# A hybrid attention layer on one core: first tile normalised in halves, rotary queries gated, narrower first scores, an offset added by DMA, the last residual placed in PSUM

## The chip, the core and the metric

The kernel runs on one core of one Trainium2 chip. The metric is device time in microseconds (us) of one execution; lower is better. Columns of a profile row are: start, duration, engine, line of the kernel, operation, output tile <- input tiles, sizes. PE is TensorE (PEld its weight loads), DVE is VectorE, ACT is ScalarE, POOL is GpSimd, SP is SyncE, which here only issues DMAs. A letter q behind an engine's name means its queue.

## The reference, cut to what matters

One decoder layer over 512 tokens with 1024 channels, float32. The input is normalised; gated linear attention and multi-head latent attention run on the same stream, are merged by gates and projected; then come a residual with layer norm (LN1), a squared-ReLU MLP of width 4096, and a residual with layer norm (LN2).

```
h = layer_norm(x, ln_in_g, ln_in_b)
mix = token_mixer(h, cos, sin, w_in, ..., w_q_b, ..., w_out)
h = layer_norm(DEEPNORM_ALPHA * h + mix, ln1_g, ln1_b)
ff = jnp.square(jax.nn.relu(h @ w_ff1)) @ w_ff2
h = layer_norm(DEEPNORM_ALPHA * h + ff, ln2_g, ln2_b)

# latent attention, 8 heads, blocks of 128 queries, block blk reads keys [0, 128 * (blk + 1))
s = einsum(q_nope[q0:q1], k_nope[:q1]) + einsum(apply_rope(q_rope)[q0:q1], k_rope[:q1])
p = softmax(where(mask, s * scale, -inf))
o = einsum(p, v[:q1])
```

## The kernel before, in words

**Number format.** Every large product is done in fp32r, a reduced form of float32. Each operand is split into a high and a low part (hi, lo), and a product is three matmuls: hi by hi, hi by lo, lo by hi. Weights come by DMA on SP's queue into three raw buffers; `pump` (L177) splits them one or two pieces ahead of use: ACT copies the high part (L189, tile whi or xh), DVE subtracts to get the low part (L190, tile wlo or xl). There are two buffers for each part, so a piece's split waits until TensorE has done with the piece two before.

**Order of the work.** The program is written as a main line of matrix products (`gemm_fm`, `gemm_tm`, which put 512 or fewer output columns in one PSUM bank) with side tasks, generators that `tick` moves on by a step between matmuls. The framework then sets each engine's order from a simulated time line and the order of the program. On the chip each engine executes its own list strictly in that order. `tc.issue_after(ins)` holds the instructions of its block behind `ins` if they are on the same engine as `ins`. PSUM has eight banks, four in a pool mm and four in a pool px; ring buffers in SBUF are given by tag. One tag, C, has eight buffers, for h0, qn, PT1, res, bc, T1 and T2.

**Start.** x has four tiles of 128 tokens. Tiles 0 and 1 come first, then the first weights. `ln_in0` (L437) normalises both through `ln_rows` (L400): statistics on DVE (L403, L404), epsilon (L405), the power -1/2 on POOL (L406), then for tile 0 a scalar nmr on DVE (L409) and one ACT instruction of 1024 columns (L410), for tile 1 one DVE instruction (L412). `ln_transpose` (L414) then transposes both tiles on TensorE (L421), 128 channels at a time, and makes h high (ACT, L424) and low (DVE, L428 and L429). The first projection (L278 to L280) follows.

**Rotary queries.** `mla_qr` (L813) projects the rotary part of four heads' queries for four token tiles into two PSUM banks; `ev_qr` (L816) multiplies each tile with cosine and sine on DVE (L498 to L500, reading PSUM), adds on POOL (L501), and splits the sum (L114, L115). The next main product, `y_gla` (L1098, matmuls L245 to L247 on ogT), needs four accumulators, so also the two banks of the queries.

**Scores.** `mla_head` (L859) computes for block i of 128 queries scores against max(128 (i + 1), 256) keys in five fp32r matmuls (L871 to L875), adds the mask by a bf16 matmul (L876), and takes the softmax over 128 (i + 1) keys.

**LN1's residual.** After LN1, `residual1` (L1193) keeps alpha times the normed stream for the second residual: the gain and offset rows bg and bb (tile bc) are multiplied by alpha (L1197, L1198), each of the four res tiles is multiplied by bg (L1199, L1203), and bb is added (L1204), all on DVE. Beside it, `win_sums` (L1234) combines quarters of w_ff2 (L1239) into T1 and T2; its second half takes the two buffers of tag C that bg and bb leave. The MLP's second product, `win_f2` (L1270), adds its results into res by accumulating DMAs from POOL's queue (L1305).

**End.** The last quarter of the second product is done by token tiles. For the last tile, three column groups of 512, 256 and 256 are accumulated (L1413 to L1415); after each, DVE adds the residual in SBUF (L1417) and takes statistics by 256 columns (L1419). `ln2` (L1208) then merges the statistics (L1215), adds epsilon (L1216), takes the power on POOL (L1217), and in two halves computes (r - mean) * gain (L1220) and times the power plus offset (L1221), and sends each half out on SP (L1222).

Of the kernel before, what the change touches and what calls it, by code (L numbers as in the profile page):

```python
# [19 lines left out]
P = 128  # L20
# [32 lines left out]
def tile_hybrid_block(ctx: ExitStack, tc: tile.TileContext, I, out, dbg=None):  # L53
# [23 lines left out]
    def B(shape, dt=F32, n="b"):  # L77
        return pb.tile(shape, dt, tag="B", name=nm(n))

    def S(shape, dt=F32, n="s"):  # L80
        return sm.tile(shape, dt, tag=n, name=nm(n))
# [5 lines left out]
    def MM(n="mm"):  # L87
        return pm.tile([P, T], F32, tag="mm", name=nm(n))
# [121 lines left out]
    def spawn(g):  # L210
        active.append(g)
        return g
# [187 lines left out]
    def ln_rows(src, dst, mv, on_act=False):  # L400
        bst = S([P, 2, 6], F32, "bst")
        for j in range(2):
            nc.vector.bn_stats(bst[:, j, :], src[:, j * T:(j + 1) * T])  # L403
        nc.vector.bn_aggr(mv, bst)  # L404
        vts(mv[:, 1:2], mv[:, 1:2], LN_EPS, None, op0=ALU.add)  # L405
        gtt(mv[:, 1:2], mv[:, 1:2], mhalf[:, 0:1], op=ALU.pow)  # L406
        if on_act:
            nmr = S([P, 1], F32, "nmr")
            stt(nmr, mv[:, 0:1], -1.0, mv[:, 1:2], op0=ALU.mult, op1=ALU.mult)  # L409
            act(dst, src, AF.Identity, scale=mv[:, 1:2], bias=nmr)  # L410
        else:
            vts(dst, src, mv[:, 0:1], mv[:, 1:2], op0=ALU.subtract, op1=ALU.mult)  # L412

# [21 lines left out]
    hT = []  # L435

    def ln_in0():  # L437
        for tt in range(2):
            ln_rows(xt[tt], xt[tt], mvin[:, tt, :], on_act=tt == 0)
        yield from ln_transpose(xt, g_in, b_in, hT, 0, alt=True)  # L440

    pump(-1)
# [370 lines left out]
    def mla_qr(g):  # L813
        qst = []

        def ev_qr(a, j, ps):  # L816
            src = ps[:, :4 * ROPE].rearrange("p (h c) -> p h c", c=ROPE)
            csb = cs2[:, a, None, :].to_broadcast([P, 4, ROPE])
            snb = sn2[:, a, None, :].to_broadcast([P, 4, ROPE])
            t1 = B([P, 4, ROPE], F32, "rt1")  # L820
            t2 = B([P, 4, ROPE], F32, "rt2")
            rope(src, csb, snb, t1, t1, t2)
            q2 = B([P, 4, 2, ROPE], F32R, "q2")
            split(t1, q2[:, :, 0, :], q2[:, :, 1, :], scale=scale)
            qst.append(q2)
        gemm_tm([PL["qr", g]], qlT, 4 * ROPE, ev_qr)

        def tr():
            for h in range(4):
                p = PX(dt=F32R)  # L830
                for tt in range(NT):
                    nc.tensor.transpose(p[:, tt * P:(tt + 1) * P], qst[tt][:, h].rearrange("p a b -> p (a b)"), identr)
                yield
                q = B([P, T], F32R, "QS")
                act(q, f(p), AF.Copy)
                QS[4 * g + h] = q
        return spawn(tr())
# [21 lines left out]
    def mla_head(h, hl, qn, kn, vt):  # L859
        for _ in range((0 if h == MH - 1 else STAG) * hl):  # L860
            yield
        KK, qs = KKs[0], QS[h]
        Ps = []
        P02 = B([P, T], F32, "P02")
        for i in range(NT):
            n = P * (i + 1)
            nn = max(n, 2 * P)
            c = slice(i * P, (i + 1) * P)
            p = PX()
            o = p[:, :nn]  # L870
            mm(o, qn[:, 0, c], kn[:, 0, :nn], start=True, stop=False)  # L871
            mm(o, qn[:, 0, c], kn[:, 1, :nn], start=False, stop=False)
            mm(o, qn[:, 1, c], kn[:, 0, :nn], start=False, stop=False)
            mm(o, qs[:, c], KK[:, 0, :nn], start=False, stop=False)
            mm(o, qs[:, c], KK[:, 1, :nn], start=False, stop=False)  # L875
            mm(p[:, c], identb, negb, start=False, stop=True)  # L876
            mx = S([P, 1], F32, "mx")
            nc.vector.tensor_reduce(mx, p[:, :n], axis=AX.X, op=ALU.max, negate=True)
            Pm = P02[:, :P] if i == 0 else P02[:, P:] if i == 2 else B([P, T], F32, "Pm")
            sme = S([P, 1], F32, "sme")  # L880
            act(Pm[:, :n], p[:, :n], AF.Exp, bias=mx, accum_out=sme)
            nc.vector.reciprocal(sme, sme)
            vts(Pm[:, :n], Pm[:, :n], sme, None, op0=ALU.mult)
            Ps.append(Pm)
            if i != 0:
                yield

        PT = [A([P, 2, T], F32R, "PT0"), A([P, 2, T], F32R, "PT1"), B([P, 2, 256], F32R, "PT2")]
        plan_t = ([(i, 0, i) for i in range(4)], [(i - 1, 1, i) for i in range(1, 4)] + [(3, 3, 3)],
                  [(i - 2, 2, i) for i in range(2, 4)])  # L890
        for b, (pl, pt) in enumerate(zip(plan_t, PT)):
            n = len(pl) * P
            p = PX()
            for cc, j, i in pl:
                nc.tensor.transpose(p[:, cc * P:(cc + 1) * P], Ps[i][:, j * P:(j + 1) * P], ident)
            split(p[:, :n], pt[:, 0, :], pt[:, 1, :])
            if b != 1:
                yield
        PT0, PT1, PT2 = PT
        while vt[NT - 1] is None:  # L900
            yield
        o = PX()
        for j in range(NT):
            c = slice(hl * P, (hl + 1) * P)
            vh, vl = vt[j][:, 0, c], vt[j][:, 1, c]
            if j == 0:
                ph, pl, od = PT0[:, 0, :], PT0[:, 1, :], o
            elif j == 1:
                ph, pl, od = PT1[:, 0, :384], PT1[:, 1, :384], o[:, 128:]
            elif j == 2:  # L910
                ph, pl, od = PT2[:, 0, :], PT2[:, 1, :], o[:, 256:]
            else:
                ph, pl, od = PT1[:, 0, 384:], PT1[:, 1, 384:], o[:, 384:]
            mm(od, vh, ph, start=j == 0, stop=False)
            mm(od, vh, pl, start=False, stop=False)
            mm(od, vl, ph, start=False, stop=j == NT - 1)
        yield
        om = A([P, 2, T], F32R, "omT")
        st["om"] = split(o, om[:, 0, :], om[:, 1, :])
        omT[h] = om  # L920
# [272 lines left out]
    def residual1():  # L1193
        bg, bb = bcast_row("ln1_g"), bcast_row("ln1_b")
        yield
        with tc.issue_after(st["ln"][1].ins):
            vts(bg, bg, ALPHA, None, op0=ALU.mult)  # L1197
            vts(bb, bb, ALPHA, None, op0=ALU.mult)  # L1198
            vtt(res[0], res[0], bg, op=ALU.mult)  # L1199
        yield  # L1200
        for tt in range(NT):
            if tt:
                vtt(res[tt], res[tt], bg, op=ALU.mult)  # L1203
            vtt(res[tt], res[tt], bb, op=ALU.add)  # L1204
            yield


    def ln2(tt, bst=None):  # L1208
        mv = S([P, 2], F32, "mv")
        r = res[tt]  # L1210
        if bst is None:
            bst = S([P, 2, 6], F32, "bst")
            for j in range(2):
                nc.vector.bn_stats(bst[:, j, :], r[:, j * T:(j + 1) * T])
        nc.vector.bn_aggr(mv, bst)  # L1215
        vts(mv[:, 1:2], mv[:, 1:2], LN_EPS, None, op0=ALU.add)  # L1216
        gtt(mv[:, 1:2], mv[:, 1:2], mhalf[:, 0:1], op=ALU.pow)  # L1217
        for j in range(2):
            c = slice(j * T, (j + 1) * T)
            stt(r[:, c], r[:, c], mv[:, 0:1], bg[:, c], op0=ALU.subtract, op1=ALU.mult)  # L1220
            stt(r[:, c], r[:, c], mv[:, 1:2], bb[:, c], op0=ALU.mult, op1=ALU.add)  # L1221
            nc.sync.dma_start(out[tt * P:(tt + 1) * P, c], r[:, c])  # L1222
        yield
# [115 lines left out]
    for ci in range(FC):  # L1339
# [34 lines left out]
        else:  # L1374
# [29 lines left out]
            gemm_tm(PL["f2last"], hid, T, ev_res, tts=(2,))  # L1404
            spawn(ln2(2))
            tt, r, bst = 3, res[3], S([P, 4, 6], F32, "bst4")
            for c0, n in ((0, T), (T, 256), (T + 256, 256)):
                acc = MM()[:, :n]
                ws = slice(c0 % T, c0 % T + n)
                for k in range(nb):  # L1410
                    hi, lo = weights(PL["f2last"][c0 // T], k)
                    xh, xl = hid[k][:, 0, tt * P:], hid[k][:, 1, tt * P:]
                    mm(acc, xh, hi[:, ws], start=k == 0, stop=False)  # L1413
                    mm(acc, xh, lo[:, ws], start=False, stop=False)
                    mm(acc, xl, hi[:, ws], start=False, stop=k == nb - 1)  # L1415
                    tick(None)
                vtt(r[:, c0:c0 + n], acc, r[:, c0:c0 + n], op=ALU.add)  # L1417
                for j in range(c0 // 256, (c0 + n) // 256):
                    nc.vector.bn_stats(bst[:, j, :], r[:, j * 256:(j + 1) * 256])  # L1419
            finish(spawn(ln2(3, bst)))  # L1420


# [46 lines left out]
```

## Time and profile before

| | |
|---|---|
| three runs, us | 896.37, 896.48, 897.16 (median 896.48) |
| the profiled execution, us | 896.5 |
| its span in the profile, us | 894.7 |
| granted TensorE clock | 0.998 |
| first projection matmul, last matmul start, us | 11.62, 887.36 |
| DMA moved | 109.41 MB, mean 122 GB/s |

The span is the time from the first to the last instruction in the trace; 1.8 us of the execution lie around it. The profile lists waits as "engine, tile, line <- engine, tile, line that ended the wait: us in total, times, longest". Ends of matmuls are modelled and overlap their successors, so how close matmuls follow is read from their starts: 512 columns are usually 0.227 us apart, 256 columns 0.12.

### The profile page before, as it was taken

To read this page: it belongs to the slowest core of one execution; us is meant where nothing else is said; L and a number is where in the kernel's file an instruction comes from. 1 tells how busy PE (TensorE), PEld (TensorE's weight loads), DVE (VectorE), ACT (ScalarE), POOL (GpSimd) and SP (SyncE) were. 2 spreads that over 40 slices of the span, in tenths; PEclk is the share of its full clock that TensorE was granted. 3 is DMA by queue.
4 is the path that set the end of the run, shared out by engine and by line. 5 is a ranking of instruction groups with operands and counts; after the bars stand their busy time and mean duration, and the time that the engine had idled before them with its cause. 6 is when DMAs were issued, how large, how long until landed. Compare 5 with 4: busy or idle time off the path is not lost.

```text
span 894.7 us, 12542 instructions
## 1 busy us (share of the span) xinstructions
PE 877.5 (98%) x4796; PEld 760.5 (85%) x4796; DVE 614.5 (69%) x1003; ACT 445.1 (50%) x757; POOL 170.4 (19%) x190
## 2 busy tenths in 40 slices
PE   6999999999999999999999999999999999999996
PEld 5988888888889988888888888988888888889986
DVE  7835855577775745747756797997556646787866
ACT  6455543443546543535645423366457546656810
POOL 1003442444531010100000002103400520141000
PEclk9999999999999999999999999999999999999999
DMA  7314413216325723112207618004950991399312
GB/s 246 122 47 163 131 60 95 71 48 152 84 71 175 197 87 102 49 55 58 95 25 260 210 48 305 3 0 118 314 135 3 271 257 35 76 231 236 117 62 82
DMA packets 73037, 109.41 MB, mean 122 GB/s; under 512 B 7904, under 2 KB 42080, under 8 KB 72976
## 3 DMA queue, kind: packets, MB, share of 16 engines
q1 hardware_dynamic: 57520, 76.62, 27.1%
q0 software_dynamic: 13536, 28.32, 13.8%
q10 hardware_dynamic: 1920, 3.66, 1.2%
q8 instruction: 38, 0.62, 0.3%
q14 instruction: 23, 0.19, 0.1%
HBM read 91.28 MB, written 4.72 MB: 107 GB/s over the span
## 4 chain that ended last, share of the span: by engine, by line
PE 97%; DVE 1%; DMA 1%; ACT 0%; issue 0%; DVEq 0%
PE mm L245 12%; PE mm L247 12%; PE mm L246 12%; PE mm L278 7%; PE mm L279 7%; PE mm L280 7%; PE mm L1030 3%; PE mm L1029 3%; PE mm L1028 3%; PE px L1288 2%; PE px L1287 2%; PE px L1286 2%; PE px L738 2%; PE mm L1288 2%; PE mm L1287 2%; PE mm L1286 2%
## 5 line engine op out<-in xcount | busy, mean ns | idle before, releaser
L190 DVE TENSOR_TENSOR wlo<-wraw,whi 128x1024 fp32r<-128x1024 f32 (+1 forms) x98 | 110.4, 1127 | 110.0 <-ACT whi L189 102.4
L189 ACT ACTIVATE whi<-wraw 128x1024 fp32r<-128x1024 f32 (+1 forms) x98 | 93.9, 959 | 97.9 <-PE mm L246 48.9
L245 PE MATMUL mm<-h,whi 128*128 128x512 f32 x288 | 112.7, 392 | 0.0
L246 PE MATMUL mm<-h,whi 128*128 128x512 f32 x288 | 112.4, 390 | 0.0
L247 PE MATMUL mm<-h,wlo 128*128 128x512 f32 x288 | 107.1, 390 | 0.0
L1305 POOL DMA_DIRECT2D res<-ev x42 | 37.4, 1003 | 177.9 <-ACT ev L1303 143.6
L245 PEld LDWEIGHTS mm<-h,whi 128*128 128x128 f32 x288 | 54.0, 188 | 11.0
L246 PEld LDWEIGHTS mm<-h,whi 128*128 128x128 f32 x288 | 54.1, 188 | 10.8
L247 PEld LDWEIGHTS mm<-h,wlo 128*128 128x128 f32 x288 | 53.9, 188 | 11.0
L279 PE MATMUL mm<-wlo,h 128*128 128x512 f32 x128 | 50.3, 393 | 0.0
L280 PE MATMUL mm<-whi,h 128*128 128x512 f32 x128 | 50.1, 392 | 0.0
L190 DVE TENSOR_TENSOR wlo<-wq,whi 128x1024 fp32r<-128x1024 f32 x30 | 36.7, 1225 | 19.4 <-ACT whi L189 19.4
L278 PE MATMUL mm<-whi,h 128*128 128x512 f32 x128 | 49.7, 403 | 0.0
L677 POOL TENSOR_TENSOR rp<-rp 128x256 f32<-128x256 f32 x32 | 31.6, 988 | 61.1 <-ACT E L682 44.8
L189 ACT ACTIVATE whi<-wq 128x1024 fp32r<-128x1024 f32 x30 | 31.7, 1058 | 19.7 <-PE mm L1029 11.4
L189 ACT ACTIVATE xh<-wraw 128x1024 fp32r<-128x1024 f32 (+1 forms) x28 | 27.4, 984 | 27.8 <-PE mm L280 16.3
L684 DVE TENSOR_TENSOR M<-E,qk 128x512 f32<-128x512 f32 x32 | 27.8, 868 | 14.1 <-ACT E L682 14.1
L406 POOL TENSOR_TENSOR mv<-mv,mhalf 128x1 f32<-128x1 f32 x4 | 4.6, 1155 | 172.3 <-DVE mv L405 172.3
L190 DVE TENSOR_TENSOR xl<-wraw,xh 128x1024 fp32r<-128x1024 f32 (+1 forms) x28 | 31.3, 1130 | 8.5 <-ACT xh L189 8.4
L1028 PE MATMUL mm<-sh,whi 128*128 128x256 f32 x128 | 36.2, 283 | 0.0
L1029 PE MATMUL mm<-sh,whi 128*128 128x256 f32 x128 | 36.2, 283 | 0.0
L1030 PE MATMUL mm<-sh,wlo 128*128 128x256 f32 x128 | 36.2, 283 | 0.0
(419 smaller groups left out, 2576.9 us busy)
## 6 DMA issues: line engine op xcount, KB each, us to landing
wraw<-in_w_in_dram SPq DMA_DIRECT2D x38, 512.0 KB, 3.5
wraw<-in_w_ff_dram SPq DMA_DIRECT2D x36, 512.0 KB, 5.1
wq<-in_w_ff_dram POOLq DMA_DIRECT2D x26, 512.0 KB, 9.7
res<-ev POOLq DMA_DIRECT2D x42, 256.0 KB, 9.2
wraw<-in_w_o_gla_dram SPq DMA_DIRECT2D x8, 512.0 KB, 3.7
wraw<-in_w_o_mla_dram SPq DMA_DIRECT2D x8, 512.0 KB, 3.5
wraw<-in_w_out_dram SPq DMA_DIRECT2D x8, 512.0 KB, 3.8
wq<-in_w_in_dram SPq DMA_DIRECT2D x6, 512.0 KB, 6.1
```

Of the source, the lines that this page charges most:

```text
L189: st["ins"] = act(hi[:, :nk, :n], raw[:, :nk, :n], AF.Copy)
L190: st["lo"] = vtt(lo[:, :nk, :n], raw[:, :nk, :n], f(hi[:, :nk, :n]), op=ALU.subtract)
L245: mm(o, hi[:, c], xh, start=first, stop=False)
L246: mm(o, hi[:, c], xl, start=False, stop=False)
L247: mm(o, lo[:, c], xh, start=False, stop=last)
L278: mm(o, xh, hi[:, :n], start=opens, stop=False, skip_group_check=share)
L279: mm(o, xh, lo[:, :n], start=False, stop=False, skip_group_check=share)
L280: mm(o, xl, hi[:, :n], start=False, stop=last, skip_group_check=share)
L1028: mm(oa, hi[:, k, c], xh, start=opens and k == 0 and a == 0, stop=False, skip_group_check=True)
L1029: mm(oa, hi[:, k, c], xl, start=False, stop=False, skip_group_check=True)
L1030: mm(oa, lo[:, k, c], xh, start=False, stop=k == 3, skip_group_check=True)
L1305: nc.gpsimd.dma_start(res[tt + t][:, j * T:(j + 1) * T], e, accum_op=ALU.add)
```

## The change

Five edits that touch different places:

1. Tile 0's last normalising instruction on ACT is done in two halves of 512 columns. All DVE instructions of tile 1's normalisation are put behind tile 0's nmr.
2. In `ev_qr`, at the first token tile the weights' split is pumped on by one piece, and the rotary products of each tile on DVE are put behind the last low part that was split.
3. The scores of the first 128 queries are computed against 128 keys, no longer 256.
4. The offset bb is added to each res tile by an accumulating DMA from SBUF to SBUF on POOL's queue, no longer by DVE.
5. For the last 256 columns of the last token tile, the residual is copied by ACT into the PSUM bank beforehand, behind the last weight split, and the matmuls accumulate onto it. The statistics, and the first step of `ln2` for these columns, read PSUM. For this tile that first step is done in column groups of 768 and 256, both ahead of the second step; for the other tiles in two groups of 512, now also both ahead of the second step.

```diff
@@ ln_rows
         if on_act:
             nmr = S([P, 1], F32, "nmr")
-            stt(nmr, mv[:, 0:1], -1.0, mv[:, 1:2], op0=ALU.mult, op1=ALU.mult)
-            act(dst, src, AF.Identity, scale=mv[:, 1:2], bias=nmr)
+            end = stt(nmr, mv[:, 0:1], -1.0, mv[:, 1:2], op0=ALU.mult, op1=ALU.mult)
+            for j in range(2):
+                c = slice(j * T, (j + 1) * T)
+                act(dst[:, c], src[:, c], AF.Identity, scale=mv[:, 1:2], bias=nmr)
+            return end
@@ ln_in0
-        for tt in range(2):
-            ln_rows(xt[tt], xt[tt], mvin[:, tt, :], on_act=tt == 0)
+        end = ln_rows(xt[0], xt[0], mvin[:, 0, :], on_act=True)
+        with tc.issue_after(end.ins):
+            ln_rows(xt[1], xt[1], mvin[:, 1, :])
@@ ev_qr
+            if a == 0:
+                pump(PL["qr", g]["idx"][-1] + 1)
             t1 = B([P, 4, ROPE], F32, "rt1")
             t2 = B([P, 4, ROPE], F32, "rt2")
-            rope(src, csb, snb, t1, t1, t2)
+            with tc.issue_after(st["lo"].ins):
+                rope(src, csb, snb, t1, t1, t2)
@@ mla_head
-            nn = max(n, 2 * P)
...
-            o = p[:, :nn]
-            mm(o, qn[:, 0, c], kn[:, 0, :nn], start=True, stop=False)
...
+            o = p[:, :n]
+            mm(o, qn[:, 0, c], kn[:, 0, :n], start=True, stop=False)
...
@@ residual1
-            vtt(res[tt], res[tt], bb, op=ALU.add)
+            nc.gpsimd.dma_start(res[tt], bb, accum_op=ALU.add)
@@ ln2
+        w = T if end is None else D - 256
+        for src, c in ((r[:, :w], slice(0, w)), (r[:, w:] if end is None else end, slice(w, D))):
+            stt(r[:, c], src, mv[:, 0:1], bg[:, c], op0=ALU.subtract, op1=ALU.mult)
         for j in range(2):
             c = slice(j * T, (j + 1) * T)
-            stt(r[:, c], r[:, c], mv[:, 0:1], bg[:, c], op0=ALU.subtract, op1=ALU.mult)
             stt(r[:, c], r[:, c], mv[:, 1:2], bb[:, c], op0=ALU.mult, op1=ALU.add)
@@ the last token tile
+            end = PX()[:, :256]
+            with tc.issue_after(st["ins"].ins):
+                act(end, r[:, D - 256:], AF.Copy)
             for c0, n in ((0, T), (T, 256), (T + 256, 256)):
-                acc = MM()[:, :n]
+                last = c0 > T
+                acc = end if last else MM()[:, :n]
...
-                    mm(acc, xh, hi[:, ws], start=k == 0, stop=False)
+                    mm(acc, xh, hi[:, ws], start=k == 0 and not last, stop=False, skip_group_check=last)
...
-                vtt(r[:, c0:c0 + n], acc, r[:, c0:c0 + n], op=ALU.add)
-                for j in range(c0 // 256, (c0 + n) // 256):
-                    nc.vector.bn_stats(bst[:, j, :], r[:, j * 256:(j + 1) * 256])
-            finish(spawn(ln2(3, bst)))
+                if not last:
+                    vtt(r[:, c0:c0 + n], acc, r[:, c0:c0 + n], op=ALU.add)
+                    acc = r[:, c0:c0 + n]
+                for j in range(n // 256):
+                    nc.vector.bn_stats(bst[:, c0 // 256 + j, :], acc[:, j * 256:(j + 1) * 256])
+            finish(spawn(ln2(3, bst, end)))
```

## The prediction

> **What bounds the kernel now.** I read the busy table first, then the chain that ended last, then the waits of TensorE.
>
> ```profile
> PE 877.5 (98%) x4796; PEld 760.5 (85%) x4796; DVE 614.5 (69%) x1003; ACT 445.1 (50%) x757; POOL 170.4 (19%) x190
> PE 97%; DVE 1%; DMA 1%; ACT 0%; issue 0%; DVEq 0%
> PE px L421 <- ACT x L410: 8.3, 1, 8.3
> PE px L738 <- DVE SD L694: 0.5, 1, 0.5
> PE mm L247 <- DVE wlo L190: 0.5, 1, 0.5
> PE mm L278 <- ACT h L424: 0.4, 1, 0.4
> PE mm L245 <- ACT h L424: 0.3, 1, 0.3
> ```
>
> TensorE holds 97% of the chain, and after its first input it waits visibly four times. Adding up the starts of all its matmuls beyond each shape's usual spacing gives about 3 us of lost time between 13 us and the last matmul at 887.36 us. So DVE, ACT or POOL work is worth nothing here unless TensorE waits for it. An edit can win in the first 13 us, at a named wait, in matmul time itself, or in the 7 us after the last matmul. All sums are made against the profiled execution, 896.5 us (span 894.7 and 1.8 around it), which is the median of the three runs shown, 896.48.
>
> **Part 1, the first tile.** The reader should see three times on DVE in the timeline:
>
> ```profile
> 6.21 0.69 DVE L403 BATCH_NORM_STATS2 bst<-x 128x6 f32<-128x512 f32 x1 [0.31 <-DMA x<-in_x_dram]
> 6.82 0.14 DVE L409 SCALAR_TENSOR_TENSOR nmr<-mvin 128x1 f32<-128x1 f32 x1
> 8.67 0.98 DVE L412 TENSOR_SCALAR x<-x,mvin 128x1024 f32<-128x1024 f32 x1 [0.67 <-POOL mvin L406]
> ```
>
> The first tile's power on POOL ends at 6.54, but nmr starts at 6.82 because the second tile's statistics went ahead at 6.21. The gate turns that round: nmr at about 6.58, so ACT starts 0.24 earlier (7.00 to 6.76) and, in two halves (512-column ACT rows take 0.6, so the two cost about what the 1.24 row did), releases the first four transposes near 7.4 rather than 8.29. But every operation on the second tile now stands behind nmr: statistics from 6.64 rather than 6.21, its L412 at 9.10, 0.43 late, and behind it on DVE the three xl splits (from 9.57) and the first lnt (12.02). TensorE's first projection matmul, at 11.62, waits for h on ACT, which stands behind a split at 10.31 that had waited for a weight load; the earlier transposes gain nothing there. The late lnt does cost: the transposes at 12.99 had their weight load held until lnt was done. The matmuls just ahead start 0.30 apart, from 14.25 on 0.165 apart, so 0.43 lost there is about 0.43 x 0.165/0.30 = 0.24 of full-speed work. I take **+0.2**. Bounds: -0.5 (h gets ahead of the split of 0.80 at 10.31) to +0.9 (an xl split also slips in front of L412).
>
> **Part 2, rotary queries.** Columns: start, duration, engine.
>
> ```profile
> 319.19 1.06 ACT L189 ACTIVATE whi<-wraw 128x1024 fp32r<-128x1024 f32 x1 [1.85 <-PE mm L280]
> 320.03 0.42 DVE L498 TENSOR_TENSOR rt<-mm,cs 128x256 f32<-128x256 f32 x1 [2.96 <-PE mm L280]
> 320.77 2.89 DVE L190 TENSOR_TENSOR wlo<-wraw,whi 128x1024 fp32r<-128x1024 f32 x2
> 321.13 0.40 PE L246 MATMUL mm<-ogT,whi 128*128 128x512 f32 x1
> 322.04 0.73 PE L247 MATMUL mm<-ogT,wlo 128*128 128x512 f32 x2 [0.51 <-DVE wlo L190]
> ```
>
> The weights' high part was ready at 320.25; DVE was in the rotary products of the first token tile (320.03 to 320.85), so the low part came late and L247 started 0.91 after L246 where 0.227 is usual: 0.68 lost. With the gate, the low part runs from about 320.3 to 321.45 and L247 can go at 321.5: **-0.6** (bounds -0.7 and 0). What waits now: the rotary products stand behind two splits (the second ends near 322.95), with the PSUM banks that y_gla's third and fourth accumulators need. Twelve matmuls of 0.227 per weight block on the two free banks cover 320.4 to about 326; the four tiles of products, about 0.8 of DVE each from 322.95, end near 326.5, where the trace had 327.33. What is late next is thus the fourth bank, needed at about 326.7. The second group (364 to 372) shows no wait of TensorE, so it gains nothing. SP's weight loads wait for the splits and so move forward with them.
>
> **Part 3, 128-column scores.** Five matmuls a head, eight heads, go from 256 to 128 columns. No score of this size is in the trace; the nearest rows are the last products with the values, same types, a weight load each:
>
> ```profile
> 378.74 0.28 PE L916 MATMUL px<-PT,mv 128*128 128x256 f32 x1
> 378.86 0.22 PE L914 MATMUL px<-PT,mv 128*128 128x128 f32 x1
> 378.92 0.28 PE L915 MATMUL px<-PT,mv 128*128 128x128 f32 x1
> 379.03 0.28 PE L916 MATMUL px<-PT,mv 128*128 128x128 f32 x1
> 379.14 0.30 PE L895 MATMUL px<-ca,P 128*128 128x128 f32 x1
> ```
>
> 256 columns are spaced 0.12; at 128 the first spacing is 0.06 and the next are 0.11, which is the spacing of the weight loads beside them (378.86, 378.97). So a head saves 0.06 + 4 x 0.01 = 0.10, eight heads **-0.8**. Bounds: 0, and 40 x 0.06 = -2.4 if every one moved at the first spacing. TensorE has no wait between 355 and 465, where these lie, so the saving counts in full. The Trainium skill, TensorE: Matmul & The Clock Gate, Back-to-back issue gap, gives about 81 ns per 128-column matmul with its weight load; by that the estimate would be 40 x (0.120 - 0.081) = 1.6, and the total 894.0. The trace's 0.11 for these types speaks against it, and I keep it out of the sum.
>
> **Part 4, LN1 offset by DMA.** Four additions of 1.22 (L1204, 579.56 to 585.3) leave DVE. TensorE has no wait for DVE between 570 and 887, so this is **0**. Added: four 512 KB accumulates, 0.86 of POOL each to issue by the res<-ev rows, on a POOL idle from 564 to 613.7 and with the DMA engines at 3 and 0 GB/s in the slices from 559 to 604. A new wait comes: the second half's T2 (DVE, 591.39) takes the buffer of the offset, free only when the last accumulate has landed, and DVE works in order, so behind it stand the w_ff2 splits. DVE reaches T2 at 591.39 - 4 x 1.14 = 586.8 now. The last accumulate is issued near 580.5 (the fourth product with the gain ends at 579.64); with the 9.2 us of the median res<-ev it lands at 589.7, so DVE stands still for 3 of its 4.6 us gained and is still ahead of the old time.
>
> **Part 5, the last residual.**
>
> ```profile
> 887.67 0.42 DVE L1417 TENSOR_TENSOR res<-mm,res 128x256 f32<-128x256 f32 x1 [1.99 <-PE mm L1415]
> 888.13 0.43 DVE L1419 BATCH_NORM_STATS2 bst<-res 128x6 f32<-128x256 f32 x1
> 889.19 0.92 POOL L1217 TENSOR_TENSOR mv<-mv,mhalf 128x1 f32<-128x1 f32 x1 [9.32 <-DVE mv L1216]
> ```
>
> With the residual already in PSUM the addition goes and the statistics start where it did: **-0.46** (888.13 - 887.67), and everything behind is moved whole. The multiply of L1220 in 768 + 256 columns costs what 512 + 512 do (0.744 at 512 and 1.284 at 1024 give 1.05 ns a column, so 1.01 + 0.47 against 1.49). Statistics from PSUM are not in the trace; maxima of 256 columns from PSUM take 0.42, so I leave 0.43, bounds -0.5 to -0.3. The copy into PSUM, about 0.4 by ACT's 256-column rows, goes on an ACT that is idle from 856.8 and is needed at 884.6.
>
> **Sum.** +0.2 - 0.6 - 0.8 + 0 - 0.46 = -1.66: 896.5 - 1.7 = **894.8 us**.
>
> **Rivals.**
> 1. *The middle gives nothing.* The order on each engine is set anew, and the waits that are left (1.4 us around 244, 0.8 around 566) show that one late split is enough; if the fourth bank comes late or new waits of this size eat parts 1 to 3, only the tail is left: 896.5 - 0.46 = 896.0. For it: a wait of 0.7 is what part 2 takes away, and such sizes come and go with the order. Against: DVE is 31% idle and relieved. Chance 0.30.
> 2. *Slower: the accumulates come late.* Place: T2 at the head of DVE's queue. TensorE needs the first w_ff2 low part (end 599.64) at 602.42 and the next (604.29) at 606.50, so DVE may lose 2.2 against the old order; the price begins when the last accumulate lands after 591.4 + 2.2 = 593.6. The longest landing of a res<-ev is 17.5: 580.5 + 17.5 = 598, price 4.4, total 894.8 + 4.4 = 899.2. For it: 512 KB is twice those transfers. Against: the DMA engines are empty, and the shortest landing was 3.3. The Trainium skill, DMA: Bandwidth & Descriptors (the fit per DMA of about 2.0 us and 436 KB a us), would put a 512 KB transfer at an estimated 3.2 us; the trace has no lone one to test it. Chance 0.12.
> 3. *More than forecast.* The scores at the 0.06 spacing throughout (-2.4) and h ahead of the split (-0.5): 896.5 - 2.4 - 0.5 - 0.6 - 0.46 = 892.5. For it: the single 0.06 spacing. Against: the 0.11 beside it. Chance 0.10.
> 4. The forecast: 0.48, its own range 893.9 to 895.8.
>
> **The numbers.** What a measurement of this kernel can tell from no change is about 0.2%, 1.8 us, so faster is below 894.7 and slower above 898.3. The forecast stands at that edge: 0.30 of its 0.48 goes to faster, rival 3 adds 0.10, some of rival 1 if only one gain is lost 0.04: faster 0.44. Slower is rival 2: 0.12. Same is the rest, 0.44. The range takes in rivals 1 and most of 3 and leaves out the price of rival 2: 893.0 to 897.4.
>
> **What would show it.** In the changed profile: nmr ahead of the second tile's statistics and L412 near 9.1; no wait of L247 near 321; 128-column scores spaced 0.11 on TensorE; T2 waiting for a DMA on DVE, with no wait of TensorE at 602 to 607; statistics 0.02 to 0.05 after the last matmul's end and the last L1221 about 0.46 nearer to it. Wrong would be: a TensorE wait of over 1 us that was not there before, score matmuls spaced 0.12 or more, or an h at 11.6 and later on ACT.

## The result, and the profile after

The changed kernel takes 899.43 us (median of eight runs, 898.24 to 900.98), beside 897.12 us for the kernel before in the same comparison. The ratio is 1.0025, with a 95% interval of 1.0016 to 1.0033: it is **slower by about 2.3 us**. That lies above the predicted range (893.0 to 897.4), on the side that had been given 0.12. The profiled span went from 894.7 to 897.5 us, the granted clock is 0.998 in both.

The same two lines of the page as before, busy time and the chain that ended last:

```profile
PE 878.0 (98%) x4796; PEld 760.6 (85%) x4796; DVE 608.0 (68%) x998; ACT 446.6 (50%) x759; POOL 172.8 (19%) x194
PE 91%; DVE 4%; DMA 3%; issue 1%; ACT 1%; POOLq 0%; DVEq 0%; ACTq 0%
```

TensorE held 97% of the chain and now holds 91%. DVE's share went from 1 to 4% and DMA's from 1 to 3%, although DVE has 6.5 us less to do. These shares are not the size of a loss: followed back in time, the chain leaves TensorE from 579.98 to 594.26 us and from about 776 to 812, and the second stretch, the longer one, ends in the smaller wait. The answer on TensorE's waits names the places:

```profile
PE mm L247 <- DVE wlo L190: 2.3, 1, 2.3
PE px L424 <- DVE x L415: 0.9, 1, 0.9
...
PE px L1036 <- DVE wlo L190: 0.4, 1, 0.4
```

There is one wait of 2.3 us that was not there, plus one of 0.9 in the first tile and one of 0.4 late in the kernel. (Lines behind the first hunk are shifted: L410 is now L412, L421 is L424, L1239 is L1247, L1305 is L1313, L1417 is L1430.)

Adding up by the starts of matmuls, after against before: 1.00 later at 124 us (125.11 for 124.11), still 0.99 later at 322, 0.47 won at L247 there, 0.70 won between 322 and 566, 2.43 lost at 592 and 0.57 at 812. That makes 2.83 of the 3.09 by which the last matmul is later (887.36 to 890.44); the rest is in steps below 0.2 each. Behind the last matmul 0.35 is won (7.37 to 7.02, by the unrounded spans of 894.73 and 897.46). 3.09 - 0.35 is the 2.74 between these spans.

**The 2.43.** DVE's timeline around it:

```profile
589.57 1.23 DVE L1247 TENSOR_TENSOR T<-wq,wq 128x1024 f32<-128x1024 f32 x1 [4.50 <-DMA res<-bc]
...
592.99 1.22 DVE L190 TENSOR_TENSOR wlo<-wraw,whi 128x1024 fp32r<-128x1024 f32 x1
```

and TensorE's:

```profile
591.60 0.39 PE L246 MATMUL mm<-h,whi 128*128 128x512 f32 x1
594.26 0.73 PE L247 MATMUL mm<-h,wlo 128*128 128x512 f32 x2 [2.28 <-DVE wlo L190]
```

T2 (the row T<-wq,wq) stood still 4.50 us for the last accumulate, which was issued at 579.98 and landed 9.46 later, at 589.44. Behind T2, in DVE's order, come six short instructions and then the low part of a w_ff1 piece, which is done at 594.2. TensorE wanted it at 591.83 (0.227 after 591.60). In the kernel before, this low part stood *ahead* of T2:

```profile
590.25 1.23 DVE L190 TENSOR_TENSOR wlo<-wraw,whi 128x1024 fp32r<-128x1024 f32 x1
591.39 1.23 DVE L1239 TENSOR_TENSOR T<-wq,wq 128x1024 f32<-128x1024 f32 x1
```

The framework set the order anew, and T2 moved forward past it. The DMA engines in the stretch between; the last three columns are granted clock, DMA share and GB/s:

```profile
577.00:589.00 12.00, 12.00 (x67) 10.46 (x66) 7.03 (x10) 6.98 (x13) 3.17 (x4) 1.00 0.93 176
```

The four accumulates fill the DMA engines for twelve microseconds by themselves; before, the same stretch had a share of 0.00 and 1 GB/s.

### The profile page after: what moved, and what is told of

Same layout as the page of the kernel before. It is cut to its first block, busy times and chain, and to the rows that moved or that the text cites. A ratio compares the mean times of both kernels' runs of the same rounds, so it can differ in the third digit from the quotient of the medians.

```text
span 897.5 us, 12544 instructions
## 1 busy us (share of the span) xinstructions
PE 878.0 (98%) x4796; PEld 760.6 (85%) x4796; DVE 608.0 (68%) x998; ACT 446.6 (50%) x759; POOL 172.8 (19%) x194
## 4 chain that ended last, share of the span: by engine, by line
PE 91%; DVE 4%; DMA 3%; issue 1%; ACT 1%; POOLq 0%; DVEq 0%; ACTq 0%
PE mm L247 12%; PE mm L245 12%; PE mm L246 12%; PE mm L278 7%; PE mm L280 7%; PE mm L279 7%; PE mm L1036 2%; PE mm L1035 2%; PE mm L1034 2%; PE px L1294 2%; PE px L1295 2%; PE px L1296 2%; PE px L742 2%; DMA res<-ev 1%; PE mm L1296 1%; PE mm L1294 1%
## 5 line engine op out<-in xcount | busy, mean ns | idle before, releaser
L246 PE MATMUL mm<-h,whi 128*128 128x512 f32 x288 | 112.4, 390 | 0.0
L247 PE MATMUL mm<-h,wlo 128*128 128x512 f32 x288 | 107.4, 390 | 2.3 <-DVE wlo L190 2.3
L1313 POOL DMA_DIRECT2D res<-ev x42 | 38.6, 1037 | 163.1 <-ACT ev L1311 126.2
L247 PEld LDWEIGHTS mm<-h,wlo 128*128 128x128 f32 x288 | 53.9, 188 | 13.7 <-DVE wlo L190 2.7
L246 PEld LDWEIGHTS mm<-h,whi 128*128 128x128 f32 x288 | 54.1, 188 | 10.8
```

What stands on the lines that cost most here:

```text
L246: mm(o, hi[:, c], xl, start=False, stop=False)
L247: mm(o, lo[:, c], xh, start=False, stop=last)
L1313: nc.gpsimd.dma_start(res[tt + t][:, j * T:(j + 1) * T], e, accum_op=ALU.add)
```

## The experiments

The reason stated first is this: the offset's DMA makes T2 wait, T2 keeps the w_ff1 split waiting, and that is the whole loss; the other four parts gain together. Rivals: the accumulates cost by their load on the DMA engines, or another part costs. Each timed run is beside the kernel before on the same chip.

**Part 4 alone.**

```diff
-            vtt(res[tt], res[tt], bb, op=ALU.add)
+            nc.gpsimd.dma_start(res[tt], bb, accum_op=ALU.add)
```

> Only part 4 (the LN1 offset by DMA) on the kernel before. Theory (the wait for the accumulate at T2 is the loss): T2 of the second half stands still on DVE until about 589.5, and TensorE waits some 2.4 us near 591 to 594; the time is 897.1 + 2.4 = 899.5. Rival (the loss is the first tile and a new order elsewhere): no TensorE wait of over 1 us near 592, time 897.1 within 0.7.

901.32 us, ratio 1.0053 (1.0040 to 1.0066): this part alone loses more than the whole change. The last accumulate landed 10.22 after its issue at 580.04, T2 ran at 590.38, and TensorE's rows are:

```profile
591.64 0.39 PE L246 MATMUL mm<-h,whi 128*128 128x512 f32 x1
595.07 0.99 PE L247 MATMUL mm<-h,wlo 128*128 128x512 f32 x2 [3.04 <-DVE wlo L190]
...
596.72 0.63 PE L247 MATMUL mm<-h,wlo 128*128 128x512 f32 x1
...
599.06 0.39 PE L247 MATMUL mm<-h,wlo 128*128 128x512 f32 x1
```

3.20 is lost at 595.07. Then matmuls of 512 columns start 0.42 to 0.43 apart, for 0.227, until 598.8: nine of them in 3.75 us, 1.7 more than at the usual spacing. The granted clock in this stretch is 0.54. Together that is 4.9, and the time shows 4.85 (901.32 for 896.47). This second loss, a slower TensorE after the wait, did not follow the 2.28 us wait of the changed kernel.

**All but part 4.**

```diff
-            nc.gpsimd.dma_start(res[tt], bb, accum_op=ALU.add)
+            vtt(res[tt], res[tt], bb, op=ALU.add)
```

> The changed kernel with part 4 undone (offset added by DVE again). Theory: the 2.4 us at 592 and the 0.6 us near 812 go, 899.4 - 3.0 = 896.4. Rival: the first tile's 1.0 and the new order stay the loss and the time is 898.5 to 899.5.

895.70 us, ratio 0.9990 (0.9982 to 0.9999). No wait at 592 and none at 812, last matmul at 886.23. Without this part the change is a small gain, only just clear of no change.

**Part 1 alone.**

```diff
+            for j in range(2):
+                c = slice(j * T, (j + 1) * T)
+                act(dst[:, c], src[:, c], AF.Identity, scale=mv[:, 1:2], bias=nmr)
...
+        with tc.issue_after(end.ins):
+            ln_rows(xt[1], xt[1], mvin[:, 1, :])
```

> Only part 1 (halves and gate) on the kernel before. Theory (the gate delays the second tile by 0.4 and TensorE warms up later): TensorE's first full-speed projection matmuls 0.4 to 1.0 later, time 897.1 + 0.4 to 1.0 = 897.5 to 898.1. Rival (the 1.0 us seen in the changed kernel's start was a late landing of x in that one execution): time 897.1 within 0.3.

897.32 us, ratio 1.0007 (0.9998 to 1.0016), so not told from no change by the time. In this one trace TensorE is 0.82 behind at 124 us and 0.86 at the last matmul.

**Parts 2, 3 and 5.**

```diff
+            with tc.issue_after(st["lo"].ins):
+                rope(src, csb, snb, t1, t1, t2)
...
-            nn = max(n, 2 * P)
+            nn = n
...
+            end = PX()[:, :256]
+            with tc.issue_after(st["ins"].ins):
+                act(end, r[:, D - 256:], AF.Copy)
```

> Parts 2, 3 and 5 (gated rotary queries, 128-column scores, residual in PSUM) on the kernel before. Theory (the parts are worth what the changed trace showed, 0.5 + 0.7 + 0.3): 897.1 - 1.5 = 895.6. Rival (the gains are eaten by waits elsewhere once the order is set anew): 896.5 to 897.1, with new TensorE waits of 0.5 or more in the trace.

895.38 us, ratio 0.9986 (0.9977 to 0.9995). Against the run of all but part 4, in the same comparison, this puts part 1 at 895.70 - 895.38 = +0.32 beside the others; the two intervals overlap, so this is not clear of noise.

**Part 4 with T2 later in DVE's order.** The transfers are the same; only T2's place is edited. `st["lo"]` is the last low part written ahead of it in the program.

```diff
-            held(t2, q12, WQ[("f2", ci), ("11", hf)], op=ALU.add)
+            with ExitStack() as late:
+                if hf and ci == 0:
...
+                    late.enter_context(tc.issue_after(st["lo"].ins))
+                held(t2, q12, WQ[("f2", ci), ("11", hf)], op=ALU.add)
```

> The kernel before with the offset added by DMA, and with the second half's T2 held on DVE behind the weight split that was last issued ahead of it in the program; its buffer is still the offset's. Theory (the loss is T2's place in DVE's queue, with the w_ff1 split behind it): T2 starts after 591.4, past the landing of the last accumulate (near 590), waits for no DMA, the w_ff1 low part is done ahead of it, TensorE has no wait above 0.6 us near 592, and the time is that of the kernel before, 896.5 (896.0 to 897.0); the 4.85 us that this edit cost alone are gone. Rival (the four accumulates themselves cost it, by loading the DMA engines at about 200 GB/s from 577 to 589 while weights and w_ff2 quarters are fetched): the transfers are the same, so a TensorE wait of 2 to 3 us stays near 592 and the time stays above 899.

896.53 us beside 896.60, ratio 0.9999 (0.9991 to 1.0008): the 4.85 are gone. DVE's rows:

```profile
588.51 1.23 DVE L190 TENSOR_TENSOR wlo<-wraw,whi 128x1024 fp32r<-128x1024 f32 x1 [0.68 <-ACT whi L189]
...
598.72 1.22 DVE L1239 TENSOR_TENSOR T<-wq,wq 128x1024 f32<-128x1024 f32 x1
```

The low part runs at 588.51, T2 at 598.72 without a wait, and TensorE goes through 592 at its usual spacing. The accumulates landed as late as ever (5.9 to 10.0 us after issue). So their load costs TensorE nothing here; the place of the waiting instruction was the loss. It also confirms the other half of the step: four additions less on DVE gain nothing.

**Part 4 with a buffer of its own for T2.** To make room, the pool of small tiles gives up two of its 22 buffers.

```diff
-    pb = ctx.enter_context(tc.tile_pool(name="pb", bufs=22))
+    pb = ctx.enter_context(tc.tile_pool(name="pb", bufs=20))
...
-            t2 = WQ[("f2", ci), ("T2", hf)] = A([P, 2, T], F32, "T2")
+            t2 = WQ[("f2", ci), ("T2", hf)] = A([P, 2, T], F32, "T2b" if hf else "T2")
```

> The kernel before with the offset added by DMA, and with a buffer of its own for the second half's T2 (the small-tile pool gives up two of 22 buffers for it), so that T2 waits for no accumulate. Theory (the wait for the buffer is the whole loss): T2 moves up to about 582 on DVE with no DMA wait, no TensorE wait near 592, time 896.0 to 897.0. Rival (load of the DMA engines, or accumulates that land late for someone else): a TensorE wait of 2 us or more stays between 585 and 620, time above 898.5. If taking the four additions off DVE is worth something by itself, it shows here as a time under 896.0.

911.93 us, ratio 1.0177 (1.0163 to 1.0191), which neither theory had. T2 went at 582.51 with no wait, and TensorE has no new wait until 629 us, as the theory had it. But then:

```profile
PE mm L1286 <- ACT ev L1303: 5.6, 3, 2.6
PE px L1286 <- ACT ev L1303: 5.0, 5, 2.3
```

The second product's evictions (ev) come late, and in this kernel ACT waits 26.9 us, in 19 waits, for earlier evictions to be added into res by DMA. In the kernel before ACT waits 30.5 us for that without holding TensorE. The likely cause is the two buffers that were taken away; the smaller pool was not run by itself. As a test of the DMA the run counts only up to 629 us.

**Part 1, halves without the gate.**

```diff
-            act(dst, src, AF.Identity, scale=mv[:, 1:2], bias=nmr)
+            for j in range(2):
+                c = slice(j * T, (j + 1) * T)
+                act(dst[:, c], src[:, c], AF.Identity, scale=mv[:, 1:2], bias=nmr)
```

> The kernel before with tile 0's normalising ACT instruction in two halves, without the gate on tile 1. Both parts together put TensorE 0.82 us behind at 124 us (124.93 for 124.11), with matmuls 0.30 apart until 15.5 us and not until about 13.8. Theory one (the gate makes tile 1 late, and the gap of 0.89 us that TensorE then has between the first and the second transposes puts off its full speed): without the gate the second transposes come at 9.7 as before, the gap is about 0.45 us, full speed comes by 14.2, and TensorE is within 0.2 us of the kernel before at 124 us; time 896.2 to 896.8. Theory two (the earlier start of the first transposes is what puts off full speed, since it makes a gap at all): full speed at 15 us or later, 0.6 to 0.9 behind at 124 us, time 897.1 to 897.4.

899.83 us, ratio 1.0038 (1.0024 to 1.0052). Theory one fits the speed (full by 14.4 us, with a gap of 0.30) and fails on the time. But the first transposes were not early here (8.38, for 8.29 before): nmr stood behind statistics that waited for x until 6.73, where it was 6.21. So the run does not tell what an early start does. Of the 3.33 us by which the last matmul is later, some 2.5 are two waits that neither theory had:

```profile
PE mm L280 <- DVE h L432: 1.3, 1, 1.3
PE mm L278 <- ACT h L427: 1.1, 1, 1.1
```

They stand at 20.78 and 32.84 us, where tiles of h come late. On ACT a weight split at 11.20 now stands between two evictions of h, which may be why. The edit itself is two instructions for one; the order that was set anew around it costs more.

**Part 1, the gate without halves.**

```diff
...
+        end = ln_rows(xt[0], xt[0], mvin[:, 0, :], on_act=True)
+        with tc.issue_after(end.ins):
+            ln_rows(xt[1], xt[1], mvin[:, 1, :])
```

> The kernel before with tile 1's normalisation gated behind tile 0's nmr, the normalising ACT instruction whole. Theory one (a gap of about 0.9 us puts off full speed): first transposes near 8.1, second near 10.1, a gap of about 0.5 us, so TensorE is nearer to the kernel before than the two parts together: 0.2 to 0.5 behind at 124 us (the late lnt is left). Theory two (the gap matters whatever its length) or a rival (only the lateness of tile 1 matters): 0.8 behind at 124 us, time 897.1 to 897.4.

897.74 us, ratio 1.0012 (1.0003 to 1.0021), and 0.99 behind at 124 us. The gap before the second transposes was 1.27 rather than 0.5, since a weight split on DVE (9.11) slipped in front of tile 1's last instruction (9.93). That is the upper bound that the prediction had named. Matmuls stayed 0.30 apart until 16.0. Since the gap came out long, the run does not tell the two theories on its length apart.

**All five parts, T2 later.** The edit is that of the held T2, on the changed kernel.

```diff
+                    late.enter_context(tc.issue_after(st["lo"].ins))
```

> The changed kernel with all five parts, and the second half's T2 held on DVE behind a later weight split, as in the run with the offset's DMA and the held T2. Theory (the whole loss of the changed kernel is T2 ahead of the w_ff1 split; the other four parts do what they did without the DMA): no TensorE wait above 0.6 us near 592 and none near 812, time that of the changed kernel without the DMA, 895.7 (895.2 to 896.2). Rival (the parts disturb each other in other ways, so that the order set anew brings a wait elsewhere): above 896.8, with a TensorE wait of over 1 us that the kernel before does not have.

895.83 us, ratio 0.9989 (0.9980 to 0.9997): as with part 4 left out (895.70). Neither the wait at 592 nor that at 812 is there. The loss of the changed kernel is the place of one instruction.

**Parts 2, 3 and 5, the short step first.**

```diff
-        for src, c in ((r[:, :w], slice(0, w)), (r[:, w:] if end is None else end, slice(w, D))):
+        for src, c in ((r[:, w:] if end is None else end, slice(w, D)), (r[:, :w], slice(0, w))):
```

> Parts 2, 3 and 5 alone, with the 256 columns that stand in PSUM taken ahead of the 768 in the first step of the last tile's LN2. With the 768 first, POOL's power of 128x1 took 1.19 us for 0.92 and ended 0.41 after the 768-column DVE instruction, and DVE's second step started 1.45 after the first step's start where the two instructions' own starts would give 1.33. Theory (POOL's power is held only while the DVE instruction runs that it started beside): the power ends 0.41 after the 256-column instruction, so about 0.9 after the first step's start, the second step starts 1.33 after the first, and last matmul to span end is 6.94 for 7.06. Rival (each DVE instruction of this kind holds POOL): the power ends 0.41 after both, so about 1.8 after the first step's start, the second step starts 0.3 to 0.4 later than with the 768 first. Time by theory 895.3 (894.8 to 895.8), by the rival 895.7; the trace tells, the time can't.

895.49 us, ratio 0.9987 (0.9978 to 0.9996). The rows, with the last matmul at 886.50:

```profile
887.65 0.47 DVE L1223 SCALAR_TENSOR_TENSOR res<-px,mv,bc 128x256 f32<-128x256 f32 x1
888.04 1.01 DVE L1223 SCALAR_TENSOR_TENSOR res<-res,mv,bc 128x768 f32<-128x768 f32 x1
889.15 1.41 DVE L1226 SCALAR_TENSOR_TENSOR res<-res,mv,bc 128x512 f32<-128x512 f32 x2
```

Neither theory's times came. POOL's power (887.87) took 0.55 and ended 0.77 after the first step's start, where the theories had 0.9 and 1.8. Nothing was won all the same: the second step starts 0.10 after the 768 group ends, 1.50 after the first step's start rather than 1.45. Its first half reads columns that this group has just written, which is the likely reason. For part 1 there is now a second pair of runs, 895.83 - 895.49 = +0.34 beside the +0.32, but these two also differ in part 4 and in the order of the step, and again the intervals overlap.

The lowest median is thus that of parts 2, 3 and 5 without 1 and 4, 895.38 us, 1.1 below the kernel before; the times do not tell it from the versions with part 1, or with part 4 and T2 held.

## Why the prediction was wrong, point by point

**Part 4, the step that failed.** The prediction cost it at 0: "DVE stands still for 3 of its 4.6 us gained and is still ahead of the old time". The landing was right (589.7 forecast, 589.44 measured), with luck: its 9.2 us was the median of transfers of half the size, between 3.3 and 17.5. Right without luck was that T2 would wait and that DVE's freed time is worth nothing by itself. What failed is the list of what is queued behind T2. It was read from the order of the kernel before, where the w_ff1 low part stands ahead of T2, so only the w_ff2 low parts that TensorE needs at 602.42 and 606.50 were counted and the price began at a landing after 593.6. (Another w_ff1 low part, at 593.19 and wanted at 597.43, stands behind T2 there too; left out, but with 3.0 to spare, more than the 2.2 that set the price.) In the order set anew the low part that L247 wants at 591.83 stands behind T2 and six short instructions: 592.99 - 589.57 = 3.42 of work ahead of it. For L247 at 591.83 the low part had to start by 590.55, T2 by 587.1, the accumulate to land by 587.0. The threshold was 6.6 us earlier than the prediction's, and the landing passed it by 2.4, which is the wait. Rival 2 had the right mechanism and sign, with the wrong place and point; that its total of 899.2 lies near the measured 899.43 is luck, since it took a landing at 598. Its list of signs ("a TensorE wait of over 1 us that was not there before") is what came. By the Trainium skill, DMA: Bandwidth & Descriptors, Anatomy of one DMA, the estimate had been 3.2 us for 512 KB; the four here took 5.4 to 9.5 us, one behind the other.

**Part 1**, +0.2 forecast, bounds -0.5 and +0.9: every figure has the forecast sign, most are larger, and by time none is clear of noise. Beside the other parts it is 0.3 by time, alone 0.85 (0.82 in the trace), and 1.00 in the changed kernel's trace. That the gate puts L412 at 9.10 came exactly in the run of part 1 alone; in the changed kernel, where x landed later, it is 9.38. The rest of the start did not go by the forecast. In the changed kernel:

```profile
7.99 1.12 PE L424 MATMUL px<-ca,x 128*128 128x128 f32 x4 [7.99 <-ACT x L412]
...
10.42 1.12 PE L424 MATMUL px<-ca,x 128*128 128x128 f32 x4 [0.89 <-DVE x L415]
...
15.17 0.50 PE L279 MATMUL mm<-xl,h 128*128 128x360 f32 x1
15.47 0.48 PE L278 MATMUL mm<-xh,h 128*128 128x360 f32 x1
```

The early transposes leave a wait of 0.89 before the late ones, and matmuls of 360 columns are still 0.30 apart at 15.47, where the kernel before had 0.165 from 14.25. That the wait causes the late full spacing is not shown: the run of all but part 4 has the same wait (1.0) and is at 0.163 from 14.26, 0.07 behind at 124 us. The two halves on ACT were not free either: 1.52 in the run of part 1 alone, where the one row took 1.24, so the weight split behind them began at 8.27 for 8.29 in spite of the earlier start.

**Part 2**, -0.6: -0.47 in the trace. L247 now starts 0.44 after L246 for 0.91. It is not the usual 0.227 yet: L247 still waits for the same low part, which now starts as soon as ACT's high part is done (321.24) and ends at 322.50. The rotary products are out of the way, and the splitting itself is what is left.

**Part 3**, -0.8: -0.70 between 322 and 566 us. The rows have the spacing that was forecast, 0.06 and then 0.11 to 0.12:

```profile
355.14 0.22 PE L878 MATMUL px<-qn,qn 128*128 128x128 f32 x1
355.20 0.27 PE L879 MATMUL px<-qn,qn 128*128 128x128 f32 x1
355.31 0.27 PE L880 MATMUL px<-KK,QS 128*128 128x128 f32 x1
```

The 81 ns of the Trainium skill (TensorE: Matmul & The Clock Gate, Back-to-back issue gap) do not show for these types.

**Part 5**, -0.46: -0.35 to the end of the span. The statistics start 0.32 after the last matmul's start, as forecast, and the first step 1.15 after it rather than 1.60. Then 0.13 is given back: the second step starts 1.45 after the first, for 1.32.

```profile
890.76 0.43 DVE L1433 BATCH_NORM_STATS2 bst<-px 128x6 f32<-128x256 f32 x1 [0.31 <-PE px L1427]
...
892.52 0.48 DVE L1226 SCALAR_TENSOR_TENSOR res<-px,mv,bc 128x256 f32<-128x256 f32 x1
893.04 1.42 DVE L1229 SCALAR_TENSOR_TENSOR res<-res,mv,bc 128x512 f32<-128x512 f32 x2
```

It waits for POOL's power, which ended at 893.01: 1.19 for 0.92 before. The prediction priced the DVE instructions by their columns and not what stands beside them.

**The sum.** The three gains make 0.47 + 0.70 + 0.35 = 1.52 in the trace, forecast 1.86; by time they are worth 1.1 (895.38 beside 896.47). Without part 4 the forecast of -1.66 would have met -0.8.

**What stays open.** Why the framework put T2 ahead of the low part was not looked into, nor why the accumulates landed 0.8 us later alone than in the whole change. The wait at 812 goes when T2 is held. The chain enters it from late res<-ev landings (785.47 to 790.03, 4.56 us) and 20 us of DVE work without a break worth naming; how these hang together with T2 was not followed.

## What to carry to other kernels

Where a program's order is set anew by an edit, list what is queued behind a newly waiting instruction in the *new* order, or assume the nearest urgent instruction on either side of it. An in-order engine that waits for a DMA passes the wait on to everything behind it, and one place in the queue was worth some 3.3 us here, the wait at 812 included (from 2.31 above the kernel before to 0.94 below it) while the four additions saved were worth nothing. At the end of a kernel, where every 0.1 us counts, check which other engine the lengthened instruction holds up.

## What the runs showed of the hardware

- **A slower TensorE after a wait, not by its length alone.** After a loss of 3.20 us (a wait of 3.04) the spacing was 0.42 for 3.7 us, at a granted clock of 0.54 (part 4 alone); after one of 2.43 (a wait of 2.28) it was not, at 1.00. In the run with T2's own buffer two losses of 2.70 and 2.78 left the spacing at 0.227 and the clock at 1.00, and one of 2.50, at 811.8, was followed by 0.43 until past 815, at a clock of 0.50. The Trainium skill, TensorE: Matmul & The Clock Gate, What's actually happening, has the clock set by a window of about 3.4 us that runs freely, so that its phase decides; that length alone does not sort these five fits that, and no run shows the window itself. Both slow stretches followed waits shorter than 3.4 us.
- **The start differs between executions.** In kernels with the same start, full spacing came between 11.85 us (part 4 alone) and 14.9 (parts 2, 3 and 5), and TensorE stood between 123.99 and 124.52 at the same matmul. With part 1 in full it was 124.17 to 126.59 (four executions). A claim of 0.5 us on the first tile needs more than one trace, and that goes for the 1.00 of the changed kernel too.
- **POOL is held by some DVE instructions.** A power of 128x1 took 0.55 us near 6 us; 0.92 beside DVE's 512-column and 1.19 beside its 768-column first step, which read res and bc from SBUF, ending 0.41 after that instruction both times; and 0.55 again where it started beside one that read PSUM and bc. The Trainium skill, GPSIMD Engine Reference, Specifications, says that the SBUF interfaces are shared with VectorE, with contention for instructions of two SBUF inputs; these rows agree. One limit: in the last case the 768-column instruction, with its two SBUF inputs, ran beside the power from 888.04 to 888.42 and neither grew longer, so the moment of its start seems to matter. And two inputs are not the only case: in the kernel before, the power that started at 535.03 took 0.91 beside a multiply with one tile of input in SBUF (L412, 535.09).
